# Gates' products between the units of the differential attention, and the first output matrix's products inside the latent attention

## The chip, the cores and the metric

The kernel runs on one core of a Trainium2 chip. A core has TensorE (PE in the profile, with its weight loads apart as PEld), VectorE (DVE), ScalarE (ACT), GpSimd (POOL) and SyncE (SP), each with an instruction queue of its own that runs in order, and 16 DMA engines. All plain transfers of this kernel are issued from SP's queue; the indirect gathers are issued from GpSimd's. The metric is the device time of one execution in microseconds.

## What is computed

One layer over 1024 prompt tokens and 64 sample tokens of width 1024: a norm, one wide input matrix, two attention branches, a gated merge, and a mixture of single-neuron experts. Cut to what matters here:

```python
h = rmsnorm(x, norm_mix)
zq, zk, zv, zcq, zckv, zkr, zg = split(h @ w_in)
gates = sigmoid(zg).reshape(B, S, 2, 1024)
o_a = diff_attention(zq, zk, zv)      # 8 heads, two softmaxes each: p0 - lam * p1
o_a = rmsnorm(o_a, diff_subln) * (1 - lambda_init)
o_b = mla_attention(zcq, zckv, zkr)   # 16 heads on a latent of 128
merged = gates[:, :, 0] * (o_a @ w_branch_a) + gates[:, :, 1] * (o_b @ w_branch_b)
x = x + merged @ w_out
x = x + peer_ffn(rmsnorm(x, norm_ffn))  # top 16 of 128*128 experts for each of 8 heads
```

Both attentions are causal in chunks of 64 tokens; the sample tokens also see a cache of 512 past tokens.

## The kernel before

The first phase, up to some 2918 us, handles the tokens in three groups of three tiles of 128 tokens (the ninth tile is the 64 sample tokens). The text counts them as groups one, two and three; in the code g is 0, 1 and 2. Each group goes through these stages, in this order in the code:

- norm and transposes into hT, then from chunks of the input matrix of 256 columns: the latent (cq, kv), the keys, the values (stored to DRAM; the values' copy is vt at L708);
- the gates, L710 to L716: eight weight chunks, two products each. cmajor makes one product of 8 contractions over all of the group's columns, ScalarE applies the Sigmoid (L715) into a tile gt, and gt is stored to gateT in DRAM;
- the queries qd, also from cmajor;
- the differential attention, L843 to L851: for each of 8 heads the queries are split into a high and a low part (load_q, on L147 and L840), keys K and values Vt are loaded, and diff_unit runs for each token tile. A unit makes the scores (L781 to L789), the maxima on VectorE, two exponentials on ScalarE (L801), and later, by the function fin, the transposes of P (L746), their copies, and the value product (L815). The list pend holds a unit's fin back until two or three later units have made their scores;
- the norm of o_a and its transposes into oT; then the first output matrix w_a, L880 to L887: for each of eight products the gate comes back from gateT into a gt and VectorE multiplies it in, into ta;
- the latent attention (mla_unit at L914, over 8 pairs of heads; prep_pair and prep_head make a pair's queries; fin_pair ends a pair), up to L1036;
- the second output matrix w_b with its gates, L1037 to L1050, then w_out, the second norm, the router's queries and keys.

In group one a product with a weight matrix is done in three passes on a high and a low part of both operands (L153 to L155), and the low part wlo of each weight chunk is made on GpSimd (L179). In groups two and three it is one native pass per contraction (L167). Weight chunks take turns in a ring of three buffers.

Beside groups two and three run the experts' dots of the tiles before: GpSimd gathers rows of an expert table (L333) and VectorE multiplies and sums them (L358); TensorE also builds one-hot products (L406). How many of these are put between two steps of the main work is set by the function pump, which the products and the ends of units call with a number of microseconds in program order. Tiles come from pools: the exponentials' tiles P and the gates' gt share one tag with five buffers, and a buffer is free again only when the readers of the tile in it, a store among them, are done. A scheduler then sets each engine's order from the traced program.

The second phase, to 4330 us, runs the experts' output product over all tokens (L1194, L1209), and the end is a last set of gathers.

## Time and profile before

| | us |
|---|---|
| median of 3 runs | 4435.86 |
| lowest and highest run | 4433.27, 4438.95 |
| the profiled execution, its own time | 4432.89 |
| span of the profiled execution | 4431.1 |

The mean granted TensorE clock of the profiled execution is 0.906. A page of the profile gives busy time and share of the span for each engine, then busy tenths over 40 equal slices, then groups of instructions by line. The view by windows gives the same for stretches that one chooses, in microseconds from the span's start, with the granted clock of TensorE as a share of full speed (2.4 GHz) and the busy share of the DMA engines. The stretches used here are stages of the three groups:

| stage | group one | group two | group three |
|---|---|---|---|
| gates' products | 155 to 225 | 833 to 918 | from 1918 |
| queries, then differential attention | 225 to 262, to 368 | 918 to 973, to 1187 | to 2230 |
| first output matrix | in 368 to 411 | 1209 to 1259 | 2326 to 2372 |
| latent attention | | to 1579 | to 2754 |

In group three the sample heads of the differential attention and the transposes of o_a lie between 2230 and 2326.

### The profile page before, as it was taken

Reading aid. Unit: us, or ns where it says so; the run is one execution under the profiler, and the core shown is the slowest. Engines: PE = TensorE matmul, PEld = TensorE weight load, DVE = VectorE, ACT = ScalarE, POOL = GpSimd, SP = SyncE. Lnnn points to the kernel's source line nnn. Section 1 sums busy time; section 2 is a strip of 40 time slices with the busy share of each in tenths; the row PEclk is TensorE's granted clock in tenths of the full one; section 3 lists DMA queues with packets and bytes.
Section 4 is the critical chain, followed back from the end, with each engine's and each line's share of the span. In section 5 each row is a group of like instructions: output and inputs, shape, how many; then the busy total and the mean of one; then the engine's idle time right before and its main releaser. Section 6 shows DMA issues by size and latency. Waiting matters only on the chain.

```text
span 4431.1 us, 52501 instructions
## 1 busy us (share of the span) xinstructions
PE 3830.3 (86%) x17737; PEld 2924.5 (66%) x17737; DVE 3188.3 (72%) x6982; ACT 1454.8 (33%) x2872; POOL 1918.0 (43%) x1353
## 2 busy tenths in 40 slices
PE   6998989887798898897868978989999969999990
PEld 6977787555566675764546766655457858888880
DVE  5043457877888877798877887669757978777776
ACT  3354632124444512223543443032023523232320
POOL 3422240444455543144444655504433445545565
PEclk9977999987798998998869988999999989999995
DMA  5431144897687797698777868979968989899987
GB/s 176 168 101 56 56 175 148 325 338 252 233 295 276 256 356 261 219 334 311 266 247 257 280 228 295 371 259 340 347 239 320 348 307 353 329 344 322 336 316 254
DMA packets 469909, 1185.02 MB, mean 267 GB/s; under 512 B 45384, under 2 KB 220968, under 8 KB 454920
## 3 DMA queue, kind: packets, MB, share of 16 engines
q0 software_dynamic: 184320, 671.17, 42.4%
q1 hardware_dynamic: 285320, 510.50, 32.7%
q8 instruction: 140, 2.29, 0.2%
q14 instruction: 129, 1.06, 0.1%
HBM read 1075.65 MB, written 105.61 MB: 267 GB/s over the span
## 4 chain that ended last, share of the span: by engine, by line
PE 38%; DVE 11%; DMA 11%; issue 11%; POOL 5%; ACT 2%; SPq 0%; POOLq 0%; DVEq 0%; ACTq 0%
PE acc_ps L1209 15%; PE mm L167 8%; PE acc_ps L1194 5%; POOL gb L333 4%; DVE gb L358 4%; DMA gb<-in_peer_u,beidx 3%; DMA gb<-in_peer_v,beidx 3%; PE mm L406 2%; PE sc L783 1%; PE mm L815 1%; DMA gm<-in_peer_u,beidx 1%; PE sc L781 1%; DMA Vt<-out_v_p 1%; PE tp L746 1%; PE mm L940 1%
## 5 line engine op out<-in xcount | busy, mean ns | idle before, releaser
L333 POOL DMA_INDIRECT gb<-in_peer_u,beidx x934 | 1230.0, 1317 | 1552.1 <-DVE gb L358 912.8
L358 DVE SCALAR_TENSOR_TENSOR gb<-gb,h2r 128x1024 f32<-128x1024 f32 x934 | 1127.7, 1220 | 222.0 <-DMA gb<-in_peer_u,beidx 204.5
L1209 PE MATMUL acc_ps<-vhi,ahi 128*128 128x512 f32 x1408 | 439.1, 394 | 36.7 <-ACT ahi L1202 36.7
L1209 PE MATMUL acc_ps<-vhi,alo 128*128 128x512 f32 x1408 | 442.6, 395 | 0.0
L1209 PE MATMUL acc_ps<-vlo,ahi 128*128 128x512 f32 x1408 | 438.6, 394 | 0.1
L333 POOL DMA_INDIRECT gb<-in_peer_v,beidx x192 | 270.0, 1406 | 232.3 <-DVE gacc L441 142.1
L167 PE MATMUL mm<-h,wraw 128*128 128x384 f32 (+1 forms) x1024 | 321.0, 474 | 17.5 <-ACT qd L727 13.4
L1194 PE MATMUL acc_ps<-vw,aw 128*128 128x512 f32 x768 | 332.6, 593 | 0.0
L1209 PEld LDWEIGHTS acc_ps<-vhi,ahi 128*128 128x128 f32 x1408 | 265.1, 188 | 98.8 <-ACT ahi L1202 36.9
L406 PE MATMUL mm<-w,of 128*128 128x128 f32 x1792 | 273.2, 301 | 65.2 <-DVE w L400 53.8
L333 POOL DMA_INDIRECT gm<-in_peer_u,beidx x154 | 201.3, 1307 | 270.5 <-DVE gm L358 101.4
L406 PEld LDWEIGHTS mm<-w,of 128*128 128x128 f32 x1792 | 254.9, 214 | 93.2 <-issue 47.1
L441 DVE SCALAR_TENSOR_TENSOR gacc<-gb,vwgt,gacc 128x1024 f32<-128x1024 f32 x192 | 246.3, 1283 | 87.8 <-DMA gb<-in_peer_v,beidx 83.7
L1209 PEld LDWEIGHTS acc_ps<-vlo,ahi 128*128 128x128 f32 x1408 | 265.2, 189 | 60.7 <-DVE vlo L1180 0.6
L1209 PEld LDWEIGHTS acc_ps<-vhi,alo 128*128 128x128 f32 x1408 | 264.9, 188 | 60.7
L179 POOL TENSOR_TENSOR wlo<-wraw,whi 128x2048 fp32r<-128x2048 f32 (+1 forms) x42 | 186.8, 4448 | 260.7 <-ACT whi L178 255.1
L167 PEld LDWEIGHTS mm<-h,wraw 128*128 128x128 f32 x1024 | 198.9, 196 | 128.9 <-ACT qd L727 14.3
L1194 PEld LDWEIGHTS acc_ps<-vw,aw 128*128 128x128 f32 x768 | 145.2, 191 | 177.4 <-issue 176.7
L1202 ACT CAST ahi<-araw 128x1024 fp32r<-128x1024 f32 x81 | 85.0, 1049 | 515.9 <-PE acc_ps L1209 446.5
L167 PE MATMUL mm<-wraw,h 128*128 128x256 f32 (+1 forms) x960 | 228.8, 394 | 23.7 <-ACT vt L708 23.0
L1178 ACT CAST vhi<-vraw 128x1024 fp32r<-128x1024 f32 x192 | 201.1, 1052 | 109.5 <-DMA vraw<-in_peer_v 54.5
L412 ACT COPY stage<-mm 128x512 f32<-128x512 f32 (+1 forms) x224 | 125.2, 560 | 339.8 <-PE mm L406 323.6
(381 smaller groups left out, 7473.0 us busy)
## 6 DMA issues: line engine op xcount, KB each, us to landing
vraw<-in_peer_v SPq DMA_DIRECT2D x192, 512.0 KB
wraw<-in_w_in SPq DMA_DIRECT2D x66, 1024.0 KB
araw<-Ad SPq DMA_DIRECT2D x105, 512.0 KB
Ad<-stage SPq DMA_DIRECT2D x48, 1024.0 KB
vw<-in_peer_v SPq DMA_DIRECT2D x64, 512.0 KB
gb<-in_peer_u,beidx POOLq DMA_INDIRECT x934
wraw<-in_w_a SPq DMA_DIRECT2D x12, 1024.0 KB
wraw<-in_w_b SPq DMA_DIRECT2D x12, 1024.0 KB
```

Of the source, the lines that this page charges most:

```text
L167: PE.matmul(out, lhsT=L[0], rhs=R[0], start=start, stop=stop)
L179: G.tensor_tensor(lo[:, :n], raw[:, :n], hi[:, :n].bitcast(F32), op=ALU.subtract)
L333: G.indirect_dma_start(out=gb, out_offset=None, in_=src, in_offset=bass.IndirectOffsetOnAxis(ap=idx, axis=0))
L358: behind(V.scalar_tensor_tensor(gb, gb, 1.0, h2, op0=ALU.mult, op1=ALU.mult, accum_out=act[:, k:k + 1]))
L406: PE.matmul(pv[:, j, :], lhsT=of[:, x // 2, :, x % 2], rhs=w[:, x // 2, :, x % 2], start=True, stop=True)
L412: S.copy(stage[:, n:, (tt - t0) // 4 + q], pc[:, n:])
L441: behind(V.scalar_tensor_tensor(acc, gb, wgt[:, k:k + 1], acc, op0=ALU.mult, op1=ALU.add))
L746: PE.transpose(pv[:kw, b, :nq], P[:nq, (b0 + b) * 128:(b0 + b) * 128 + kw], ident[:nq, :nq])
L1178: S.copy(hi, raw)
L1194: PE.matmul(pst[t][:, ds], lhsT=rv[:, i, :], rhs=vb[i][:, ds], start=c == 0 and i == 0, stop=False)
L1202: S.copy(av, rv)
L1209: PE.matmul(pst[t][:, ds], lhsT=L[:, i, :], rhs=R[:, ds], start=c == (0 if ip else NWHOLE and -1) and i == 0 and L is ahi and R is vb[i][0 ...
```

## The change

The gates' stage goes away. One gate chunk of weights is loaded with each head of the differential attention, and one gate's product stands after each of the head's first two units. It is copied raw to gt and stored; the Sigmoid is applied after the gates have come back: for the first eight gates on ta in two large instructions ahead of the first output matrix, for the other eight one by one at the second. The eight gates that ta takes come by eight loads in a row. In groups two and three a product of the first output matrix no longer stands in a stage of its own: own_a(k) makes one in each head pair of the latent attention, after the last unit of the pair's first head. The key tiles of group one's attention come from the buffers of the gathers, and in groups two and three the slot lat is taken after the differential attention.

```diff
+MIXED = (0, 1, 2)
+LATE_A = True
...
-        for j in range(8):
-            w = wchunk(A["w_in"][14 + j])
-            for hh in range(2):
-                gt = ptile("gt", (128, GN))
-                p = cmajor(hT, w, hh)
-                S.activation(gt[:, :NH], p[:, :NH], AF.Sigmoid)
-                ld(gateT[g, 2 * j + hh, :, :NH], gt[:, :NH])
+        def gate(w, k):
+            gt = ptile("gt", (128, GN))
+            p = cmajor(hT, w, k % 2)
+            S.copy(gt[:, :NH], p[:, :NH])
+            ld(gateT[g, k, :, :NH], gt[:, :NH])
+
+        mixed = g in MIXED
+        if not mixed:
+            for j in range(8):
+                w = wchunk(A["w_in"][14 + j])
+                for hh in range(2):
+                    gate(w, 2 * j + hh)
...
-            K = slot3("K", 2, L_all)
+            if nat:
+                K = slot3("K", 2, L_all)
+            else:
+                K = gp.tile([128, D], F32R, name="K", tag="gb")[:, :2 * L_all].rearrange("p (a n) -> p a n", a=2)
...
-            for t in ptiles:
+            w = wchunk(A["w_in"][14 + h]) if mixed else None
+            for ui, t in enumerate(ptiles):
                 diff_unit(t, h, Q, loc[t], K, Vt, nr_, (t + 1) * 128)
+                if mixed and ui < 2:
+                    gate(w, 2 * h + ui)
...
-        for j in range(4):
-            w = wchunk(A["w_a"][j])
-            for hh in range(2):
-                k = 2 * j + hh
-                gt = ptile("gt", (128, GN))
-                ld(gt[:, :NH], gateT[g, k, :, :NH])
-                p = cmajor(oT, w, hh)
-                V.tensor_tensor(ta[:, k, :NH], p[:, :NH], gt[:, :NH], op=ALU.mult)
+        for k in range(8):
+            ld(ta[:, k, :], gateT[g, k, :, :NH])
+        for k in range(0, 8, 4):
+            S.activation(ta[:, k:k + 4, :], ta[:, k:k + 4, :], AF.Sigmoid)
+        wa = [None]
+
+        def own_a(k):
+            if k % 2 == 0:
+                wa[0] = wchunk(A["w_a"][k // 2])
+            p = cmajor(oT, wa[0], k % 2)
+            V.tensor_tensor(ta[:, k, :], p[:, :NH], ta[:, k, :], op=ALU.mult)
+
+        late_a = LATE_A and nat
+        if not late_a:
+            for k in range(8):
+                own_a(k)
+        if nat:
+            lat = slot("lat")
...
+                    if late_a and i == 0 and ui == len(tiles) - 1:
+                        own_a(hp)
...
                 ld(gt[:, :NH], gateT[g, 8 + k, :, :NH])
+                S.activation(gt[:, :NH], gt[:, :NH], AF.Sigmoid)
                 p = cmajor(bT, w, hh)
```

Three places in the order show what moves. The first is TensorE in group two's differential attention, a few units in the middle; tp are transposes, sc scores, mm over Vt value products, mm over h a gate's product. Before:

```order
L746 MATMUL tp<-identR,P_8114 128x128 x4
L781 MATMUL sc<-K,Qd 128x128
L783 MATMUL sc<-K,Qd 128x128
L781 MATMUL sc<-K,Qd 128x512
L783 MATMUL sc<-K,Qd 128x512
L789 MATMUL sc<-nearhl,identR 128x256 x2
L815 MATMUL mm<-Vt,PT 128x128 x4
L746 MATMUL tp<-identR,P_8161 128x128 x5
```

The same engine and stage after, between two units:

```order
L822 MATMUL mm<-Vt,PT 128x128
L169 MATMUL mm<-h,wraw_57 128x384 x8
L788 MATMUL sc<-K,Qd 128x128
L790 MATMUL sc<-K,Qd 128x128
L788 MATMUL sc<-K,Qd 128x512
L790 MATMUL sc<-K,Qd 128x512
L796 MATMUL sc<-nearhl,identR 128x256 x2
L753 MATMUL tp<-identR,P_8053 128x128 x6
```

A gate's eight passes now stand between the value product of one unit and the scores of another; elsewhere they are split in two by a value product.

The second is TensorE in group two's latent attention; mm over cq are a pair's queries, mm over ckv_all weighted values, L406 (L408 after) the one-hot products. Before:

```order
L746 MATMUL tp<-identR,Pm 128x128 x4
L167 MATMUL mm<-cq,wraw_55 128x384 x4
L940 MATMUL mm<-PT,ckv_all 128x128 x6
L746 MATMUL tp<-identR,Pm 128x128 x5
L406 MATMUL mm<-w,of 128x128 x4
```

After:

```order
L753 MATMUL tp<-identR,Pm 128x128 x4
L408 MATMUL mm<-w,of 128x128 x4
L169 MATMUL mm<-o,wraw_55 128x384 x8
L964 MATMUL mm<-PT,ckv_all 128x128 x5
L408 MATMUL mm<-w,of 128x128 x4
L169 MATMUL mm<-cq,wraw_57 128x384 x4
L964 MATMUL mm<-PT,ckv_all 128x128 x6
```

The product over o (the first output matrix, eight passes) now stands ahead of the weighted values that follow the transposes.

The third is SP's queue between group two's differential and latent attention; CK and lat are the latent keys, Ad a store from the dots' side. Before:

```order
L69 DMA gt<-gateT 128x384 x5
L69 DMA Ad<-stage 2048x1x128
L69 DMA CK<-ckvd 128x2x768
L69 DMA gt<-gateT 128x384
L69 DMA lat<-kpd 96x768
L69 DMA wraw_59<-in_w_a 128x2048
L69 DMA gt<-gateT 128x384
```

After:

```order
L71 DMA gateT<-gt 128x384
L71 DMA Vt<-out_v_p 128x6x128
L71 DMA Ad<-stage 2048x1x128
L71 DMA wraw_57<-in_w_mla 128x1792
L71 DMA gateT<-gt 128x384
L71 DMA Ad<-stage 2048x1x128
L71 DMA ta<-gateT 128x384 x8
L71 DMA CK<-ckvd 128x2x768
L71 DMA lat<-kpd 96x768
```

The latent keys now follow all eight loads of ta, and those follow the last store of a gate.

## Rows read from the trace of the kernel before

**Rows 1.** The page: busy time by engine, and granted clock by slice (tenths).

```profile
PE 3830.3 (86%) x17737; PEld 2924.5 (66%) x17737; DVE 3188.3 (72%) x6982; ACT 1454.8 (33%) x2872; POOL 1918.0 (43%) x1353
...
PEclk9977999987798998998869988999999989999995
```

**Rows 2.** Stages by windows: busy us of each engine, granted clock, DMA share, GB/s.

```profile
core 0: us, PE busy (x) PEld busy (x) DVE busy (x) ACT busy (x) POOL busy (x), PEclk, DMA share, GB/s
155.00:225.00 70.00, 70.00 (x399) 70.00 (x398) 0.00 (x0) 24.76 (x26) 38.38 (x9) 1.00 0.49 173
225.00:262.00 37.00, 37.00 (x207) 34.85 (x205) 18.39 (x21) 17.16 (x32) 17.16 (x4) 1.00 0.38 132
262.00:368.00 106.00, 89.87 (x304) 67.56 (x304) 46.23 (x120) 50.51 (x190) 5.96 (x2) 0.53 0.22 67
833.00:918.00 85.00, 80.95 (x251) 47.50 (x250) 81.57 (x324) 10.61 (x19) 39.98 (x35) 1.00 0.95 352
973.00:1187.00 214.00, 165.80 (x704) 122.31 (x703) 172.87 (x302) 102.78 (x256) 97.51 (x76) 0.74 0.73 250
833.00:1187.00 354.00, 295.52 (x1091) 197.44 (x1089) 285.02 (x678) 122.97 (x293) 163.92 (x132) 0.82 0.81 289
1209.00:1259.00 50.00, 49.75 (x196) 32.31 (x195) 35.55 (x58) 8.46 (x12) 25.24 (x21) 1.00 0.93 338
1209.00:1579.00 370.00, 315.34 (x1712) 238.85 (x1711) 303.10 (x499) 167.22 (x380) 201.19 (x155) 0.92 0.80 278
1918.00:2230.00 312.00, 248.87 (x1038) 172.70 (x1036) 268.67 (x653) 121.59 (x270) 133.84 (x107) 0.87 0.85 304
2326.00:2372.00 46.00, 42.92 (x194) 32.20 (x193) 33.10 (x54) 8.65 (x13) 20.95 (x18) 1.00 0.93 327
2326.00:2754.00 428.00, 365.54 (x2130) 293.38 (x2129) 334.97 (x539) 186.71 (x409) 246.60 (x169) 0.90 0.77 262
2918.00:4330.00 1412.00, 1366.72 (x5452) 996.14 (x5450) 1093.37 (x1984) 387.07 (x441) 646.26 (x472) 0.98 0.87 319
4330.00:4432.00 102.00, 0.00 (x0) 0.00 (x0) 69.83 (x106) 4.60 (x8) 49.93 (x41) 0.52 0.76 255
```

**Rows 3.** What TensorE waited for in group two's differential attention (total us, times, longest).

```profile
PE mm L815 <- DMA Vt<-out_v_p: 19.3, 4, 5.8
PE sc L781 <- ACT P L801: 15.5, 11, 2.6
```

**Rows 4.** GpSimd's instructions in group one's gates, queries and attention: busy us, mean ns.

```profile
L179 POOL TENSOR_TENSOR wlo<-wraw,whi 128x2048 fp32r<-128x2048 f32 x13 | 60.1, 4622 | 55.2 <-ACT whi L178 55.2
```

**Rows 5.** The line of the splits: ns min, median, max; first and last start.

```profile
L147 DVE TENSOR_TENSOR Qd<-qd,Qd x64: 204/540/4307, 228.9 to 2259.2; 64x384 fp32r<-64x384 f32 x32, 64x256 fp32r<-64x256 f32 x16, 64x64 fp32r<-64x64 f32 x16
...
L147 DVE TENSOR_TENSOR khl<-tp,khl x24: 476/548/690, 77.8 to 1856.0; 128x384 fp32r<-128x384 f32 x16, 128x320 fp32r<-128x320 f32 x8
```

**Rows 6.** Timelines of VectorE and GpSimd, 252 to 259 us: start, us, what.

```profile
254.16 4.89 DVE L147 TENSOR_TENSOR Qd<-qd,Qd 64x384 fp32r<-64x384 f32 x2 [1.15 <-ACT Qd L146]
...
253.42 4.63 POOL L179 TENSOR_TENSOR wlo<-wraw,whi 128x2048 fp32r<-128x2048 f32 x1 [5.90 <-ACT whi L178]
```

**Rows 7.** TensorE in group two's gates, by shape: busy us, mean ns.

```profile
L167 PE MATMUL mm<-h,wraw 128*128 128x384 f32 x251 | 81.7, 488 | 4.1 <-ACT gt L715 4.1
```

**Rows 8.** The chain of waits: start, us, what.

```profile
1030.48 11.80 DMA Vt<-out_v_p
...
1056.67 12.32 DMA Vt<-out_v_p
...
1872.51 14.24 DMA out_v_p<-vt
```

**Rows 9.** The gates' line on ScalarE: ns min, median, max; then its waits.

```profile
L715 ACT ACTIVATE gt<-mm x48: 437/484/492, 158.2 to 2000.7; 128x384 f32<-128x384 f32 x32, 128x320 f32<-128x320 f32 x16
...
L715 ACT ACT_TABLE_LOAD  x5: 1283/1283/1283, 156.2 to 1952.2; - x5
...
  DMA gateT<-gt: 9.6, 2
```

More of the change, by code (lines that the diff above doesn't have):

```diff
@@ L667, in hybrid_tile @@
         w = wchunk(A["w_in"][1])
-        lat = slot("lat")
+        if not nat:
+            lat = slot("lat")
         if nat:
@@ L672, in hybrid_tile @@
             cqT = [lat[:, 2 * a * NH:2 * (a + 1) * NH].rearrange("p (k n) -> p k n", k=2) for a in range(2)]
-        KP = lat[:, 4 * NH:4 * NH + (L_all + PAST + NS if smp else L_all)]
         for t in tiles:
@@ L879, in hybrid_tile @@
         ta = ta_slot[:, :8 * NH].bitcast(F32).rearrange("p (a n) -> p a n", a=8)
-        for j in range(4):
-            w = wchunk(A["w_a"][j])
-            for hh in range(2):
-                k = 2 * j + hh
-                gt = ptile("gt", (128, GN))
-                ld(gt[:, :NH], gateT[g, k, :, :NH])
-                p = cmajor(oT, w, hh)
-                V.tensor_tensor(ta[:, k, :NH], p[:, :NH], gt[:, :NH], op=ALU.mult)
+        for k in range(8):
[13 more added lines that the diff above has]
+        if nat:
+            lat = slot("lat")
+        KP = lat[:, 4 * NH:4 * NH + (L_all + PAST + NS if smp else L_all)]
         LK = L_all + PAST if smp else L_all
```

## The prediction

> **What bounds the kernel now.** I read the page's busy shares first, then the busy times by stage, then the views that price the pieces. Over the span TensorE is busy 86% and VectorE 72%, but these are averages over stages with different limits [rows 1]. The changed stages all lie before 2918 us. From there to 4330 TensorE is busy 1366.72 of 1412 us, and the last 102 us are gathers without a matmul [rows 2]; the order of the instructions there is the same in both kernels, so I let all of it slide by whatever the first part gains or loses, microsecond for microsecond.
>
> In the first part each group has stages with opposite needs, and the reader should see this in the columns of [rows 2]. In the gates' stage TensorE never stops (70.00 of 70 us in group one, 80.95 of 85 in group two). In the differential attention it waits on a chain: scores, maximum, exponential, transpose, value product. In group one that chain is 106 us with TensorE busy 89.87 us at a granted clock of 0.53; at full clock those 89.87 us would be about 48. In group two it is 214 us with 165.80 busy at 0.74, and the waits are for loads of the values and for exponentials [rows 3]. The two later groups also carry the router's dots: VectorE is busy 81.57 of 85 us (96%) in group two's gates, but 285.02 of 354 (81%) over gates, queries and attention together. So the bound changes from stage to stage. Mixing a dense stage with a waiting one can bring both nearer to the engine that has most work over the two. In groups two and three that is VectorE, in group one TensorE.
>
> **The change part by part.** I sum against the profiled execution: span 4431.1 us, its own time 4432.89, which is 3 us under the median 4435.86.
>
> *Gates into the attention, group one.* Removed is the stage 155 to 225; added are two gates in each head, of 24 passes each. 399 passes in 70 us are 0.175 us each, so two gates are 8.4 us a head. A head of the attention now takes 106/8 = 13.3 us and holds about 48/8 = 6 us of TensorE at full clock. Together that is 14.4 us of work a head: the gates fit into the wait almost exactly and TensorE becomes the bound. The whole stretch 155 to 368 (213 us) has a floor of 70 + 37 + 48 = 155 us, a gain of 58. I don't take the floor: the head's chain must still end, and gates stand as two blocks of 4.2 us in front of transposes that are ready. With 1 to 2 us a head lost (15.5 to 16 us) and the start and end of the chain bare, I take 178 us, **gain 35**, between 5 and 58.
>
> What holds the low end is a cost that moves too. Each gate chunk of group one needs its low part made on GpSimd, 4622 ns each [rows 4], now in the attention, eight times. VectorE's split of the queries takes 540 ns at the median and 4307 ns at the longest, while the split of the keys, which reads one operand from PSUM, never took over 690 ns [rows 5]. A pair of such splits of the queries, 4.89 us together, lies at 254.16 us beside the low part that GpSimd made from 253.42 to 258.05, and ends 1 us behind it [rows 6]. So a VectorE instruction with two SBUF operands can lose 4307 - 540 = 3.8 us to the low part. Eight of these on the path would be 30 us and leave 5 of the 35.
>
> The Trainium skill ("SBUF — State Buffer", section "Who interferes with whom") speaks against the change here: a VectorE instruction with two SBUF inputs contends with a GpSimd instruction that reads SBUF, and the later one waits for the whole of the other. The rows on the two splits agree with it. By that rule alone the sum would lose up to those 30 us; it is the third rival below.
>
> *Gates into the attention, groups two and three.* A native pass takes 488 ns [rows 7], so a gate of 8 passes is 3.9 us and two are 7.8 us a head. They move from a stage where VectorE is full into one where TensorE and VectorE both wait. Group two, 833 to 1187: VectorE's 285.02 us at the 96% of the gates' stage would be 297 us, a gain of 57. At 90% it is 317 us: **gain 37**. I take 90%, since the chain of the attention remains, and since loads of the values sit on the path at 11 to 12 us each [rows 8], which the gates can now cover. Group three, 1918 to 2230, is already at 268.67 of 312 (86%): at 96% a gain of 32, at 90% **gain 14**. Low ends: 5 and -10, if the gates delay the heads as much as they fill.
>
> *The first output matrix's products into the latent attention, groups two and three.* Removed are the stages 1209 to 1259 and 2326 to 2372, in which TensorE is busy 49.75 and 42.92 us; one product goes into each head pair. Over product stage and latent attention TensorE is busy 315.34 of 370 and 365.54 of 428 us, 85% in both. It idles 55 and 62 us, so the products would fit if the idle time came in the right places. I take 90% busy, 350 and 406 us: **gain 20 and 22**. High ends are the whole stages, 50 and 46. Low ends are -15 each: the product is put before the weighted values of the next units, and its weight chunk holds one of three ring buffers, so a late chunk makes all of the order behind it late.
>
> *The gates' loads and sigmoids.* Before, each gate was a Sigmoid of 484 ns on ScalarE, with a table load of 1283 ns now and then [rows 9]. Now the raw gates are copied, and between attention and latent attention come eight loads of 128 x 384 and two Sigmoids over half of them each; eight smaller Sigmoids follow at the second output matrix, where ScalarE waits for the products anyway, so these cost nothing (uncovered 8 x 0.48 = 4 us a group). The loads at the boundary cost something in groups two and three. The loads of the latent keys stand behind them in SP's queue, and ScalarE stands in its own queue on the Sigmoids while the first exponentials of the latent attention wait behind. Eight loads are 1.57 MB, at the 289 GB/s of group two's stretch [rows 2] 5.4 us. The two Sigmoids are at most 2 x 4 x 0.484 = 3.9 us and a table load 1.3. Some of it lies beside the last transposes; I take 8.5 us a group, **cost 17**, between 0 and 21. In group one the products still stand in one block behind the loads and cover them: **cost 2**.
>
> The key tiles that move to the gathers' buffers in group one cost nothing, since no gather runs before 757 us; if they took turns with the exponentials' tiles there, it would be one wait a head of some 1 us, inside the loss already taken.
>
> **Sum:** 35 + 37 + 14 + 20 + 22 = 128, less 19, is 109. 4432.89 - 109 = 4324, and at the median's distance **4327 us**.
>
> **The rivals.**
>
> *Gates pay, late products don't* (15%). The latent attention may be bound by its own chain and the dots, so that a product put into it lengthens it by its own time. Then the 42 are missing: 4369. For it: the latent attention is at 85% of TensorE already. Against it: 55 us of idle time in group two.
>
> *Near the floors* (10%). The gates cover the value loads fully and VectorE reaches 96%: 45 + 57 + 32 + 35 + 35, less 10, is 194: 4242. Against it: no stage with an attention in it shows such shares.
>
> *The low parts block the queries* (12%). The 30 us above: 4357. Against it: the splits for the next head can be made early, and the median of the 64 pieces shows that most escape.
>
> *Stores hold the exponentials: slower* (13%). The raw gates go through the same five buffers as the exponentials' results, and a buffer is free only when its store has landed. In the changed order 39 exponentials wait for such a landing in name, 15 of them in group one, against 22 waits of exponentials for any transfer before. ScalarE runs in order, so a held exponential also holds the copies behind it, the scores' banks and TensorE. The price: two gates in the stage of before waited 9.6 us together for their stores, 4.8 each [rows 9], and a store of values stands on the chain of waits with 14.24 us [rows 8]. The gain of 109 is eaten from 109/39 = 2.8 us each. At 3.5 us it is 136 us, 4463. Against it: a store of before was issued into a stage that filled buffers as fast as it could; here a gate comes once in a unit, and the store has some 5 us before its buffer's next turn.
>
> *Nothing net* (5%): fill and delay cancel, 4427 to 4445. That the change doesn't do what it says I exclude by the order: both stages are gone from it and the products stand inside.
>
> **How the numbers follow.** The forecast and what lies near it (4290 to 4345) have 45%. The range leaves out the slower case and the one at nothing (18%) and takes in most of the floors' case: 4250 to 4415. Faster by over 0.2% (9 us, about what a measurement of this kernel can tell from no change) is 45 + 15 + 10 + 12 = 82%, within it 5%, slower 13%.
>
> **What would show it.** In the profile after, the stretch from the end of the values' products to the end of the differential attention should be some 178 us in group one at a clock well above 0.53, some 317 in group two with VectorE near 90%, some 298 in group three. From the transposes of the output to the end of the latent attention it should be some 358 and 414 us, with the boundary's wait in it. If the waits of TensorE name exponentials that wait for the gates' stores, the slower rival is there. If the queries' splits take 4 us eight times, the third one is. A clock in group one's attention that stays near 0.53 would break the first term, since the floor there is made at full clock.

## The result

The changed kernel takes 4484.07 us (median of four runs, 4479.44 to 4487.81) against 4434.57 (4429.74 to 4438.95): ratio 1.0091, interval 1.0062 to 1.0121. It is slower by some 50 us; 4327 was forecast. The profiled executions have spans of 4431.1 and 4486.0 us, so 55 us are to be found in the traces.

The page of the changed kernel, busy time by engine and the granted clock by slice. Little in it differs from [rows 1]: nearly the same instructions and busy times, in a span that is longer.

```profile
span 4486.0 us, 52529 instructions
...
PE 3794.2 (85%) x17737; PEld 2897.7 (65%) x17737; DVE 3203.5 (71%) x6982; ACT 1465.4 (33%) x2902; POOL 1955.4 (44%) x1353
...
PEclk9988999987999898998869988999999989999995
```

The loss shows when both traces are cut at the same events: the end of the values' copies, the start of the normalisation of the differential attention's output, the last weighted value of the latent attention, the last addition of the output matrix. In us:

| stretch | before | after | difference | forecast |
|---|---|---|---|---|
| gates, queries, differential attention, group one | 212.2 | 211.5 | -1 | -35 |
| the same, group two | 370.0 | 359.3 | -11 | -37 |
| the same, group three | 403.0 | 402.4 | -1 | -14 |
| first output matrix, latent attention, group one | 175.5 | 178.4 | +3 | +2 |
| the same, group two | 373.8 | 394.2 | +20 | -20 + 8.5 |
| the same, group three | 432.2 | 455.0 | +23 | -22 + 8.5 |
| second output matrix to the output matrix, three groups | 254.1 | 265.0 | +11 | 0 |
| norms to values, three groups; all after 2831 | 2210.4 | 2220.3 | +10 | 0 |

So the gates' mixing gave 12 us instead of 86, the late products cost some 43 with the boundary instead of bringing 25, and 21 us went in stretches that I had at nothing.

The stretches of the changed kernel by windows (the columns are those of [rows 2]): gates to differential attention of the three groups, then the latent attentions of groups two and three with what stands before them.

```profile
core 0: us, PE busy (x) PEld busy (x) DVE busy (x) ACT busy (x) POOL busy (x), PEclk, DMA share, GB/s
156.00:367.00 211.00, 182.52 (x908) 162.60 (x906) 83.48 (x141) 89.32 (x245) 59.41 (x13) 0.85 0.35 115
...
839.00:1198.00 359.00, 274.04 (x1116) 179.88 (x1114) 296.89 (x709) 120.30 (x298) 172.85 (x138) 0.86 0.83 296
1198.00:1593.00 395.00, 320.29 (x1721) 240.69 (x1722) 305.18 (x499) 173.78 (x384) 206.36 (x154) 0.89 0.75 257
1943.00:2345.00 402.00, 310.87 (x1339) 216.68 (x1337) 339.08 (x789) 150.95 (x363) 177.50 (x135) 0.81 0.83 287
2345.00:2800.00 455.00, 366.16 (x2139) 298.05 (x2139) 337.30 (x541) 190.60 (x416) 265.13 (x170) 0.87 0.74 249
```

VectorE does 305.18 us of work in group two's latent stretch as before (303.10 in [rows 2]), but in 395 us: 77%, where my 350 us would have needed 87. In the gates' stretch it is at 83%, where I wanted 90.

What TensorE waited for in group two's differential attention, the answer to [rows 3] (total us, times, longest):

```profile
PE mm L378 <- DMA bsrc<-wgtd: 36.2, 1, 36.2
PE mm L408 <- DVE w L402: 9.4, 3, 6.0
PE sc L788 <- ACT P L808: 9.2, 5, 5.5
PE tp L753 <- DVE P L814: 8.3, 2, 4.2
```

The waits for loads of the values (19.3 us in [rows 3]) are gone: the gates do cover them. In their place is one wait of 36.2 us that had no row before. L378 is the transposes with which the one-hot products of an expert tile begin; they need wgtd, the finished dots of all 128 experts of that tile. Group three has the same, the first row of its waits from 1990 to 2345:

```profile
PE mm L378 <- DMA bsrc<-wgtd: 39.3, 1, 39.3
```

TensorE's timeline around the first of the two (start, us, what, and in brackets the idle time before it):

```profile
1068.11 1.09 PE L753 MATMUL tp<-identR,P 128*128 128x128 f32 x4 [0.30 <-ACT PT L759]
1105.38 0.90 PE L378 MATMUL mm<-identR,bsrc 128*128 128x128 f32 x3 [36.17 <-DMA bsrc<-wgtd]
```

And VectorE's in the same time, where 18 dots follow each other with no attention's work between them:

```profile
1071.32 1.22 DVE L360 SCALAR_TENSOR_TENSOR gb<-gb,h2r 128x1024 f32<-128x1024 f32 x1
...
1072.47 1.22 DVE L360 SCALAR_TENSOR_TENSOR gb<-gb,h2r 128x1024 f32<-128x1024 f32 x1
...
1074.89 1.26 DVE L360 SCALAR_TENSOR_TENSOR gm<-gm,h2r 128x1024 f32<-128x1024 f32 x1 [1.20 <-DMA gm<-in_peer_u,beidx]
...
1077.61 1.23 DVE L360 SCALAR_TENSOR_TENSOR gb<-gb,h2r 128x1024 f32<-128x1024 f32 x1 [1.45 <-DMA gb<-in_peer_u,beidx]
```

TensorE had run ahead with the gates and the attention, and then stood until the dots came up. VectorE takes 28 us for the 18, partly because it waits for their gathers (the brackets). 200 us after the end of the values the kernel before has finished 6 units of attention and 102 of the group's dots, the changed one 14 units and 100 dots; at 275 us it is 13 and 17 units, 128 and 133 dots (24 and 23 of them lie before the end of the values). A tile has 128. The units were faster, the dots were not.

### The profile page after: what moved, and what is told of

It is laid out like the page before. It is cut to its first block, busy times and chain, and to the rows that moved or that the text cites. A ratio compares the mean times of both kernels' runs of the same rounds, so it can differ in the third digit from the quotient of the medians.

```text
span 4486.0 us, 52529 instructions
## 1 busy us (share of the span) xinstructions
PE 3794.2 (85%) x17737; PEld 2897.7 (65%) x17737; DVE 3203.5 (71%) x6982; ACT 1465.4 (33%) x2902; POOL 1955.4 (44%) x1353
## 4 chain that ended last, share of the span: by engine, by line
PE 48%; DMA 16%; DVE 15%; issue 12%; POOL 5%; ACT 3%; SPq 1%; POOLq 0%; DVEq 0%; ACTq 0%
PE acc_ps L1236 18%; PE mm L169 10%; DMA gb<-in_peer_u,beidx 5%; PE acc_ps L1221 5%; POOL gb L335 4%; DVE gb L360 4%; PE mm L408 2%; DMA gb<-in_peer_v,beidx 2%; PE mm L155 2%; PE mm L156 2%; PE mm L157 2%; DMA out_v_p<-vt 1%; PE sc L790 1%; PE mm L964 1%; DMA gm<-in_peer_u,beidx 1%
## 5 line engine op out<-in xcount | busy, mean ns | idle before, releaser
L335 POOL DMA_INDIRECT gb<-in_peer_u,beidx x934 | 1248.8, 1337 | 1560.6 <-DVE gb L360 954.4
L335 POOL DMA_INDIRECT gb<-in_peer_v,beidx x192 | 281.0, 1464 | 218.6 <-DVE gacc L443 132.5
L408 PE MATMUL mm<-w,of 128*128 128x128 f32 x1792 | 270.9, 300 | 78.9 <-DVE w L402 51.4
L408 PEld LDWEIGHTS mm<-w,of 128*128 128x128 f32 x1792 | 250.9, 212 | 105.5 <-issue 57.1
L1221 PEld LDWEIGHTS acc_ps<-vw,aw 128*128 128x128 f32 x768 | 145.4, 191 | 178.6 <-issue 175.5
L1207 DVE TENSOR_TENSOR vlo<-vraw,vhi 128x1024 fp32r<-128x1024 f32 x192 | 229.0, 1219 | 1.9 <-ACT vhi L1205 1.8
```

The lines of the kernel that those rows point to most:

```text
L335: G.indirect_dma_start(out=gb, out_offset=None, in_=src, in_offset=bass.IndirectOffsetOnAxis(ap=idx, axis=0))
L408: PE.matmul(pv[:, j, :], lhsT=of[:, x // 2, :, x % 2], rhs=w[:, x // 2, :, x % 2], start=True, stop=True)
L1207: V.tensor_tensor(lo, raw, hi.bitcast(F32), op=ALU.subtract)
L1221: PE.matmul(pst[t][:, ds], lhsT=rv[:, i, :], rhs=vb[i][:, ds], start=c == 0 and i == 0, stop=False)
```

## The experiments

Each kernel was timed beside runs of the kernel before on its chip. Their runs spread more than those above (late_off 4421 to 4455), so one profile of groups two and three is good to about 10 us; group one, which has no dots beside it, repeats within 1 us.

**late_off, gates_back: one part of the change each.** In late_off the constant LATE_A is False; in gates_back MIXED is empty.

```diff
-LATE_A = True
+LATE_A = False
```

> The changed kernel with the first output matrix's products back in a stage of their own in groups two and three; everything else as changed. In the changed kernel the stretch from the norm of the attention's output to the end of the latent attention is 394.3 and 455.0 us, before it was 373.7 and 432.2. Theory A: the late products themselves lengthen the latent attention, so without them the two stretches fall back to some 382 and 440 (the boundary's loads and Sigmoids, 8 us each, stay) and the median is near 4455. Rival: the loss comes from the boundary and from the transfers around it, not from the products; then it stays within 10 us of 4484.

4440.61 us, ratio 0.9990 (0.9969 to 1.0010). The two stretches are 369.3 and 437.6 us. The place of the products, with what goes with it, is the loss; without it the change costs and gains nothing.

```diff
-MIXED = (0, 1, 2)
+MIXED = ()
```

> The changed kernel with the gates' products back in a stage ahead of the queries in all groups; raw gates, late Sigmoids and late products as changed. From the end of the values to the norm of the attention's output the changed kernel takes 211.4, 359.3 and 402.4 us, the kernel before 212.2, 370.0 and 403.0. Theory A: mixing brought only these 12 us, since the bound did not move, so the median is near 4496. Rival: mixing also delays what follows (stores, the order of the transfers, the late products), and without it the latent attentions shorten, to some 4460 in all.

4510.97 us, ratio 1.0143 (1.0118 to 1.0168). That is 15 over the 4496 of the first theory: mixing the gates is worth 27 us as it stands, over the 12 of the stretches (which are near the spread of a profile). The rival is out: the latent attentions do not shorten beyond the spread (399.5 and 448.2 us).

**half_before, half_after: both kernels with half of the dots.**

```diff
+        V.memset(act, 0.0)
         for k in range(ns):
+            if k % 2:
+                left["dots"] -= 1
+                yield
+                continue
             gb = gather(A["peer_u"], eidx[:, k:k + 1])
```

> The kernel before with every second of the experts' dots left out (no gather and no multiplication for it, a zero in its place), the rest and its order's pacing as before. It is the base for the next run. Some 540 gathers and dots of phase one go, and a part of phase two's; if the dots set the end of groups two and three, the median is 150 us or more under that of before, if the main work's own chain does, under 60.

4123.01 us, ratio 0.9262 (0.9239 to 0.9285): 320 us less. The dots, with their gathers, set much of the time.

> The changed kernel with every second of the experts' dots left out in the same way. Theory A: in groups two and three the dots' stream sets the end, at some 2.4 us a dot before and after, and swallows what the mixing gains; with half of them gone the gain appears, and this run is 40 to 110 us under the run of the kernel before with half of the dots. Rival: the mixing itself lengthens the chains of both attentions, with or without dots; then this run stays 20 to 60 us above it.

4126.34 us, ratio 0.9277 (0.9256 to 0.9299): with half of the dots the change is level with the kernel before, where with all of them it loses 50 us. Neither expectation holds as a whole. The stretches say why: gates and differential attention fall from 305.8 to 281.9 us in group two and from 343.9 to 329.7 in group three, so mixing gains 24 and 14 us there (11 and 1 with all dots); the latent stretch of group two still grows, 315.5 to 338.8 us, that of group three hardly (366.6 to 369.6). The window of group two's gates and attention, in half_before and then in half_after:

```profile
836.00:1142.00 306.00, 277.63 (x1113) 186.23 (x1111) 205.28 (x546) 125.83 (x299) 74.39 (x56) 0.90 0.63 211
```

```profile
836.00:1118.00 282.00, 260.53 (x1110) 171.47 (x1109) 208.51 (x556) 116.12 (x291) 72.53 (x62) 0.96 0.67 230
```

TensorE goes from 91 to 92% busy at a clock that rises from 0.90 to 0.96: where VectorE has room (67 and 74% busy here), the gates fill as I had thought.

**late_off_delay, nodep: the wait at the transposes.** Both start from late_off. late_off_delay puts ten steps of pacing ahead of the one-hot products of tiles 0 and 3; nodep takes their dependence on the dots away and so computes with wrong weights.

```diff
+        for _ in range(10 if t in (0, 3) else 0):
+            yield
         src = bp.tile([128, 3, 128], F32, name="bsrc", tag="oh1")
```

> As late_off, but the one-hot products of the first expert tile of groups two and three start later in the order: ten steps of their pacing, about two heads. In late_off TensorE stands 36.4 and 38.8 us at their transposes, until the last of the tile's dots has landed. Theory A: TensorE was only put there too early, so it fills these waits with the next heads and the two stretches of gates and attention (358.2 and 401.9 us) shorten by 15 us or more each: 4441 to some 4410. Rival: the dots' stream (2.4 us a dot, in one order with the attention's work on VectorE, and its loads ahead in SP's queue) sets the end all the same; then the wait only moves, and the two stretches stay within 5 us.

4411.98 us, ratio 0.9936 (0.9905 to 0.9968). The waits are 5.6 and 0.0 us, and the stretches of gates and attention 325.2 and 382.9 us, 33 and 19 less than in late_off. Of that, group two's latent stretch takes 31 back (369.3 to 400.5), with 79 more one-hot products in it, group three's only 7, with 80 more. Ahead of both latent stretches TensorE's longest wait is now the one for the norm of the attention's output on VectorE, which took 10.0 and 3.4 us in late_off:

```profile
PE tp L608 <- DVE o_a L891: 28.9, 1, 28.9
```

```profile
PE tp L608 <- DVE o_a L891: 25.0, 1, 25.0
```

The order was too early there, as the first theory says; a good part of the wait and of the gain moves on, as the rival says.

```diff
-        ld(src[:, 0, :], wgtd[t])
+        ld(src[:, 0, :], efd[t][:, 0, :])
```

> As late_off, but the block that waits for the tile's dots is loaded from another array that is ready early (so the weights in the one-hot products are not the computed ones). Nothing in TensorE's order then waits for the last dot of a tile. Theory A: the two waits of 36 and 39 us go and most of them is gained, below 4400. Rival: the dots set the end; TensorE runs ahead and then waits for the attention's maxima and exponentials, which stand behind the dots in VectorE's order; within 15 us of 4441.

4393.23 us, ratio 0.9898 (0.9865 to 0.9930), 47 us less than late_off, of 75 us of wait. Gates and attention take 342.2 and 386.3 us. TensorE's first rows of waits in group two are now

```profile
PE tp L753 <- DVE P L814: 15.4, 3, 6.0
PE mm L408 <- DVE w L402: 9.3, 3, 6.2
PE sc L788 <- ACT P L808: 7.3, 5, 2.2
```

These are hardly longer than in late_off (13.6, 7.4 and 7.5 us in the same stretch). Group two's stretch is 16 us shorter for 36 us of wait; no row says where the other 20 went.

**late_off_lowv: group one's low parts on VectorE.** From late_off, and only for the gates' chunks:

```diff
-        G.tensor_tensor(lo[:, :n], raw[:, :n], hi[:, :n].bitcast(F32), op=ALU.subtract)
+        (V if cur.get("lowv") else G).tensor_tensor(lo[:, :n], raw[:, :n], hi[:, :n].bitcast(F32), op=ALU.subtract)
```

> As late_off, and in group one the low part of the eight gate chunks is made on VectorE instead of GpSimd, so that no GpSimd instruction reads on-chip memory during that attention. In the changed kernel VectorE's small product sf (two operands in on-chip memory) took 3.0 to 3.3 us eight times, once beside each low part, against 0.22 us otherwise. Theory A: this block costs 3 us a head and, by the wait it makes, TensorE's clock too; the stretch from the end of the values to the norm of the attention's output falls from 211.5 to some 185 us, and the median from 4441 to some 4415. Rival: the head's own chain (three units' scores in a row, then their transposes, two gates behind) sets the 22 us a head; then the stretch stays within 4 us of 211.5.

Group one's stretch is 201.4 us (201.3 to 203.3 in the three later kernels with this edit, 211.2 to 211.5 in all kernels with mixed gates without it). The block is real and worth 10 us of the 26 expected; two of the eight remain, at 321 and 344 us, beside low parts that GpSimd still makes. The median, 4443.95 us, ratio 1.0002 (0.9982 to 1.0023), doesn't show them; whether they are given back in the groups behind or lie under the spread stays open. What the block looks like in the changed kernel, VectorE's timeline and GpSimd's:

```profile
287.70 0.17 DVE L811 RECIPROCAL rl<-lsum 128x2 f32<-128x2 f32 x1 [0.39 <-ACT o_a L824]
287.90 3.18 DVE L813 SCALAR_TENSOR_TENSOR sf<-lsum,rl,neglam 128x1 f32<-128x1 f32 x1
291.12 0.48 DVE L814 SCALAR_TENSOR_TENSOR P<-P,sf,P 128x256 f32<-128x256 f32 x1
...
286.54 4.53 POOL L181 TENSOR_TENSOR wlo<-wraw,whi 128x2048 fp32r<-128x2048 f32 x1 [18.10 <-ACT whi L180]
```

One element a partition (sf at 287.90) takes 3.18 us instead of the median's 0.22, until GpSimd is through.

**late_evac: does the late product hold its PSUM buffer too long?**

```diff
+            gt = ptile("gt", (128, GN))
+            S.copy(gt[:, :NH], p[:, :NH])
-            V.tensor_tensor(ta[:, k, :], p[:, :NH], ta[:, k, :], op=ALU.mult)
+            V.tensor_tensor(ta[:, k, :], gt[:, :NH], ta[:, k, :], op=ALU.mult)
```

> The changed kernel, with each late product of the first output matrix copied out of PSUM by ScalarE and only then multiplied by VectorE. Theory A: in the latent attention the late product holds one of two PSUM buffers until VectorE, behind dots, comes to it, and that keeps weighted values and queries waiting (ScalarE waits 82.6 us for the weighted values, before 32.9); then the copy frees it sooner and the stretches of 394.2 and 455.0 us shorten by 10 us or more each, to some 4460. Rival: it is the product's own time on TensorE, in a row in front of work that is due; then no change, 4484 within 8 us.

4492.98 us, ratio 1.0112 (1.0081 to 1.0143): no gain. Its two stretches are 382.3 and 449.8 us, 12 and 5 less than in the changed kernel, and the two ahead of them 4 and 7 more; by one profile that is near the spread. The buffer is not the loss; that it has a small part in it is not excluded.

**before_delay, delay_lowv, delay5_lowv: control and combination.** The first puts the ten steps into the kernel before; the second has late_off, the ten steps and the low parts on VectorE; the third the same with five steps.

> The kernel before with nothing but the later start of the one-hot products of the first tile of groups two and three (the same ten steps). It is the control for late_off_delay, which took 4412 against 4441 of late_off. There TensorE waits 0.0 and 5.2 us at these transposes. Theory A: the later start pays only where the mixed gates have brought TensorE ahead of the dots; here nothing, 4440 within 9. Rival: spreading the one-hot products further back into the latent attention pays by itself, whatever the gates do; then this kernel too is 15 us or more under the kernel before.

4436.28 us, ratio 0.9993 (0.9972 to 1.0014): nothing. The later start pays only together with the mixed gates.

> late_off_delay and late_off_lowv in one kernel: gates mixed, the first output matrix in a stage of its own, one-hot products ten steps later, the low parts of group one's gate chunks on VectorE. Theory A: the 29 us of the one and the 10 us that the other took from group one's attention (211.5 to 201.4) lie in different stages and add up, 4402 within 9. Rival: what group one gains is given back behind it, 4412 or more.

4422.70 us, ratio 0.9958 (0.9935 to 0.9981), not under late_off_delay: the two edits don't add up here.

> As delay_lowv with five steps instead of ten. With ten, group two's gates and attention fell to 325.2 us but its latent attention, which took over 80 of the one-hot products, rose from 369.3 to 400.5; at zero steps TensorE waits 36 us. Theory A: what counts is that the wait at the transposes is gone; five steps (about one head, 15 us) leave some 15 of the 36 us, so 4410 to 4425. Rival: the shift of work into the latent attention costs as much as the wait; then five is better than ten, under 4400.

4406.68 us, ratio 0.9928 (0.9905 to 0.9951): 32 us faster than the kernel before and 77 faster than the changed one, the fastest version found that computes the right result. It lies just outside both expectations. Its windows, gates and attention, then the latent stretch, of groups two and three:

```profile
832.00:1176.00 344.00, 278.88 (x1072) 181.99 (x1070) 284.83 (x688) 113.68 (x285) 163.85 (x134) 0.85 0.84 298
1176.00:1549.00 373.00, 318.97 (x1760) 242.44 (x1761) 317.98 (x523) 180.73 (x395) 211.79 (x160) 0.93 0.83 289
1886.00:2267.00 381.00, 305.26 (x1296) 210.89 (x1295) 332.12 (x778) 147.46 (x354) 178.44 (x135) 0.80 0.84 297
2267.00:2710.00 443.00, 369.65 (x2190) 299.56 (x2190) 345.08 (x552) 198.49 (x425) 267.88 (x170) 0.90 0.78 263
```

VectorE is at 83 and 87% in the gates' stretches and 85% in group two's latent one; nowhere near the 96% of the old gates' stage [rows 2].

**late_on_delay5: the late products put back into it.**

> As delay5_lowv (4407), but with the first output matrix's products inside the latent attention again, as in the changed kernel. Theory A: the stage of their own ran at 49.75 us of TensorE in 50, the latent attention at 85% or less; the products and the dots and one-hot products that come with them lose there what they saved and more, whatever stands ahead, so the stretches of 372.7 and 443.1 us grow by 10 to 25 us each: 4430 to 4455. Rival: they cost only because TensorE, held at the transposes, met the late weights and loads at a bad time; with that wait gone the products are at least free: 4410 or less.

4489.34 us, ratio 1.0104 (1.0063 to 1.0145): 83 us over delay5_lowv, more than either expected. The latent stretches grow from 372.7 to 407.1 and from 443.1 to 471.6 us. The late products do not cost because of the wait at the transposes: with most of it gone (3.3 and 9.0 us are left) they cost more, 83 us against 43.

**late_product_only, late_pacing_only: what of the late product costs.** Each product carries a call of pump, which puts dots and one-hot products beside it. The first kernel moves the product and leaves the calls ahead of the latent attention; the second leaves the product and moves the calls. The first:

```diff
-            p = cmajor(oT, wa[0], k % 2)
+            p = cmajor(oT, wa[0], k % 2, 0 if nat else 3.9)
...
         if nat:
+            for k in range(8):
+                pump(3.9)
             lat = slot("lat")
```

> The changed kernel, with the pacing calls of the late products (8 times 3.9 us of dots and one-hot products a group) left ahead of the latent attention, where the products stood before; the products alone stand inside. Theory A: a product among waiting work costs more there than in its own stage, whatever goes with it; 4484 within 15, well over 4441 of late_off. Rival: it is the dots and one-hot products that moved in with the products (VectorE's busy time in the latent attention of group two rose from 260 to 301 us); then most of the 44 us goes, 4455 or less.

4459.79 us, ratio 1.0027 (1.0005 to 1.0049): 24 us less than the changed kernel, 19 more than late_off. The second, with LATE_A False and the same first edit:

```diff
-                    if late_a and i == 0 and ui == len(tiles) - 1:
-                        own_a(hp)
+                    if nat and i == 0 and ui == len(tiles) - 1:
+                        pump(3.9)
```

> The other half: the first output matrix's products in a stage of their own as in late_off, but without dots and one-hot products paced beside them; these calls of the pacing stand inside the latent attention, one in each pair. Theory A: the pacing is not the cost; 4441 within 15. Rival: it is; 4465 or more.

4522.05 us, ratio 1.0181 (1.0139 to 1.0224): 81 us over late_off. Here the rival holds by far; in the first kernel the time lies just over its bound, with 24 of the 43 us between late_off and the changed kernel gone. The windows of group two's stretch from the first output matrix to the end of the latent attention, of late_off, late_product_only, late_pacing_only:

```profile
1199.00:1568.00 369.00, 311.01 (x1717) 234.28 (x1718) 305.65 (x504) 174.79 (x386) 203.42 (x155) 0.94 0.81 279
```

```profile
1196.00:1575.00 379.00, 319.07 (x1709) 239.88 (x1709) 306.02 (x503) 174.56 (x386) 205.58 (x154) 0.90 0.80 274
```

```profile
1197.00:1603.00 406.00, 333.32 (x1727) 251.03 (x1728) 309.74 (x508) 176.34 (x389) 209.14 (x156) 0.87 0.76 261
```

VectorE's work is the same 306 to 310 us in all three; where the dots, the one-hot products and the products stand differs. With the pacing in the loop the stretch is 37 us longer. In the loop itself, from the first scores to the last weighted value, late_off has 134 dots and 265 one-hot products recorded, the changed kernel 155 and 338; late_product_only has 143 and 266. The product stage and the loop apart, of late_off and then of late_pacing_only:

```profile
1199.00:1265.00 66.00, 59.38 (x227) 38.91 (x228) 44.29 (x71) 17.36 (x23) 30.08 (x22) 0.94 0.87 309
1265.00:1568.00 303.00, 251.63 (x1491) 195.37 (x1491) 261.37 (x434) 157.43 (x363) 173.35 (x133) 0.94 0.80 273
```

```profile
1197.00:1249.00 52.00, 50.08 (x163) 29.98 (x164) 9.24 (x14) 9.02 (x11) 0.00 (x0) 0.96 0.42 151
1249.00:1603.00 354.00, 283.25 (x1565) 221.06 (x1564) 300.50 (x495) 167.32 (x378) 209.14 (x156) 0.86 0.81 277
```

The stage gives up 35 us of VectorE's work and shortens by 14; the loop takes up 39 and grows by 51, with VectorE at 86 and 85%. So 35 us of VectorE's work cost 14 us beside the products, and 39 cost 51 in the loop. Which of the two, dots or one-hot products, costs more is not shown, since one call moves both. The two halves don't add up either: 81 and 19 us apart, 43 together. With the pacing in the loop already, moving the products brings 38 us (4522.05 to 4484.07), as the stage goes in which VectorE is left almost without work.

## Why the prediction was wrong

*The direction.* The forecast failed in the two steps that took a busy share at which a mixed stretch would run: 90% of VectorE for the gates (83% measured in group two), 90% of TensorE for the latent attention (81%). I took these as if the engine with the most work would fill up once the other's work was spread. But the dots are tied to the main work in one order on VectorE and, by the one-hot products, in one order on TensorE. For the late products I also looked at TensorE alone. The latent loop of the kernel before held VectorE at 84% and TensorE at 83:

```profile
1262.00:1575.00 313.00, 259.39 (x1495) 202.61 (x1495) 263.88 (x436) 156.01 (x364) 175.95 (x134) 0.90 0.78 269
```

The old product stage kept TensorE at 49.75 of 50 us and carried 35.55 us of VectorE's work beside it [rows 2]. I read that row as a stage with a bound to be relieved. Taking it apart put its dots and one-hot products into this loop. The dots by themselves went through at much the same rate in every stage of group two: 34 in the 85 us of the old gates' stage, 19 in the 50 of the product stage, 134 in the 313 of the loop.

*Gates in groups two and three (37 + 14 forecast, 11 + 1 measured).* That the gates cover the loads of the values was right: group two's row of 19.3 us is gone. The low end of 5 covered group two's result, but its reason was another: not heads that are delayed, but the next consumer, one-hot products that stand in TensorE's order at the point where, with the old speed of the units, the dots were just done. Two waits of 36 and 39 us took the place of what was gained. A wait that takes the place of the one removed is the rival that I didn't have. nodep shows what they are worth (47 us on the median, on top of late_off), half_after that with half of the dots the gain is there (24 and 14 us).

*Late products (20 + 22 forecast, a loss of 25 + 17 measured between late_off and the changed kernel).* My low end of -15 each came from the product's place ahead of due work and from its ring buffer. The step that I left out is that a moved product takes its pacing call along. I costed passes, loads and Sigmoids and put at nothing, without a reason, what comes along: some 20 dots in group two, at 1.22 us of VectorE each, and 73 one-hot products. late_pacing_only shows that these alone lengthen the two stretches by 37 and 38 us. The product itself, moved from a stage that keeps them, gains nothing and costs little: 378.8 and 434.7 us against 369.3 and 437.6, with 19 us on the median.

*Group one (35 forecast, 1 measured).* Two sizes were off, the floor and the price of the low parts. The floor of 155 us took the attention's 89.87 us of TensorE times the granted clock of 0.53, as if a pass took twice as long at half the clock. The changed kernel has the same scores at both levels, in windows with a granted clock of 1.00 and 0.50:

```profile
211.45 0.44 PE L790 MATMUL sc<-K,Qd 64*128 64x384 f32 x1
...
225.87 0.69 PE L790 MATMUL sc<-K,Qd 64*128 64x384 f32 x1
```

```profile
211.00:213.00 2.00, 2.00 (x11) 1.26 (x10) 1.11 (x4) 1.62 (x8) 0.00 (x0) 1.00 0.09 28
225.80:228.30 2.50, 2.50 (x7) 1.45 (x6) 0.05 (x1) 0.28 (x2) 0.00 (x0) 0.50 0.00 0
```

That is 1.6 times, not twice. The rows by shape don't show it, since their means mix the two levels. Before:

```profile
L815 PE MATMUL mm<-Vt,PT 128*128 128x128 f32 x96 | 25.6, 423 | 1.6 <-ACT PT L752 1.6
L789 PE MATMUL sc<-nearhl,identR 128*128 128x256 f32 x56 | 21.1, 475 | 0.0
...
L783 PE MATMUL sc<-K,Qd 64*128 64x384 f32 x14 | 9.1, 650 | 0.0
```

The same shapes in the changed kernel:

```profile
L822 PE MATMUL mm<-Vt,PT 128*128 128x128 f32 x96 | 17.7, 314 | 0.6 <-ACT PT L759 0.6
L796 PE MATMUL sc<-nearhl,identR 128*128 128x256 f32 x56 | 17.6, 404 | 0.0
L753 PE MATMUL tp<-identR,P 128*128 128x128 f32 x47 | 11.2, 331 | 20.4 <-DVE P L814 20.4
L790 PE MATMUL sc<-K,Qd 64*128 64x384 f32 x14 | 9.1, 651 | 0.0
```

The mean clock rises from 0.53 to 0.82 and the value products' mean falls from 423 to 314 ns, but the scores of 64 rows and 384 columns stay at 650 and 651: in both kernels 12 of these 14 run at the lower level. In the changed kernel they stand behind the wait for P, in which the clock falls from 1.00 to 0.50. Counted in TensorE's order, each pass from its start to the next one's, the attention without the gates still fills some 64 us in late_off_lowv and some 71 in the changed kernel, not 48. So the floor was some 175 us, and a head of 14.4 us of work was one of some 17. On top come these waits, 20.4 us in the rows above. The third rival, low parts that block VectorE, was there as a mechanism, on other victims than I named: not the queries' splits (at most 0.56 us now) but sf, eight times 3.0 to 3.3 us. Without six of these, in late_off_lowv, 12 of the 14 scores run at the upper level (mean 473 ns), and the stretch is 10 us shorter, not 30. What holds the rest of the stretch above the floor is not shown by a run.

The Trainium skill ("SBUF — State Buffer", section "Who interferes with whom") says that a VectorE instruction with two inputs in SBUF contends with a GpSimd instruction that reads SBUF. The trace agrees down to the smallest one: sf, begun at 287.90, ends at 291.08, GpSimd's low part at 291.07.

*Boundary and Sigmoids (cost 19 forecast).* Group one's 3 us fit the 2. In groups two and three late_off's stretches are 4 us shorter and 5 longer than before, so the 8.5 a group were too much there. Two stretches that I put at nothing grew by 11 and 10 us in the three groups. In the first of them, at the second output matrix, ScalarE now stands in its queue for the gates' loads (L1070 is the Sigmoid there):

```profile
  ACT gt L1070: 43.7, 13
  ACT P L808: 14.2, 4
```

But these waits are not shown to cost the 11 us: late_off has 51.7 us of them and a stretch of 257.9 us, 4 more than before, nodep 42.3 us and 253.2, 1 less. What made the rest of the 21 us stays open. The second row answers the slower rival. Exponentials that wait for the gates' stores are there, but 4 times and 14.2 us in all, not 39 times, and late_off, which is level with the kernel before, has 18.8 us of them: the result is slower, and not by that mechanism.

*What I had right:* that all after 2831 us slides by (1600.0 and 1601.3 us), that the gates cover the loads of the values, and that they gain where VectorE has room (half_after). Against late_off the late products gained in no run.

## What to carry to other kernels

Before a stage that fills one engine is broken up to cover the waits of another, look at what the other engines do beside it, and what of that goes along: here 35 us of VectorE's work stood beside the products, and the loop that it came into held VectorE at 84% already. When one stream gets faster, find the point where it meets the stream that doesn't (here the one-hot products that need the last dot) and move that meeting point too; late_off with this alone became 0.6% faster than the kernel before. And don't scale a busy time by the granted clock: take the durations at either level from the rows.

## What the runs showed of the hardware

A VectorE instruction on one element a partition is held as long as a large one: 3.18 us beside a GpSimd instruction of 4.53 us. A matmul of 64 rows and 384 columns recorded 0.44 us at a granted clock of 1.00 and 0.69 at 0.50, a value product of 128 by 128 some 0.28 and 0.42: 1.6 and 1.5 times as long at half the clock, not twice.
